# Interleaving the two experts of a pair, chunk by chunk, in a mixture-of-experts stage

## The chip, the cores and the metric

The kernel runs as one launch on one core of a Trainium2 chip. The metric is the device time in microseconds: 1492.72 us, the median of three runs (1490.94, 1492.72 and 1494.07).

## The reference, and what is computed

Two layers of a decoder for 256 tokens of width 1024, in float32. Layer 0 is a mixer of RWKV-7 and forgetting attention with a dense SwiGLU behind it; layer 1 is a causal convolution module with a mixture of experts behind it. Only the last part matters here:

```python
logits = xt @ w_router                       # 256 tokens, 8 experts
top_v, top_i = lax.top_k(logits, 2)          # two experts for each token
for e in range(8):                           # hidden width 3584
    y = y + gates[:, e:e+1] * (silu(xt @ w_gate[e]) * (xt @ w_up[e])) @ w_down[e]
```

Each expert has three matrices of 1024 x 3584 float32, so all eight have 352 MB of weights, which are read once. A token goes to two experts of eight, so an expert sees 64 tokens on average; how many each sees is known only when the router has run.

## The kernel before, in words

**Stages.** Layer 0 and the convolution take the first 575 us of the profiled execution. The expert stage (method `moe`, from L1357 on) takes the rest.

**Loads.** A weight matrix is cut into 7 chunks of 512 hidden columns; a chunk of one matrix is two loads of 1 MiB (L1221 to L1230). All loads are issued by SyncE in the program's order into a ring of 12 buffers (`wx`, `wt`, `wr`), so a load waits until what lay in its buffer has been read.

**Experts by size.** Expert 0 goes first, alone. The other seven are sorted by their number of tokens. The largest, `big`, is computed with split float32r operands: each 1 MiB load is cut into two parts, and `parts` (L1264) makes a high half `bh` on ScalarE (L197) and from it a low half `bl` on VectorE (L198). Its work is 21 *phases*, 7 chunks times gate, up and down, with two loads each; on TensorE a phase is 96 matmuls of L1279 or 48 of L1298 to L1300. The other six form three pairs of a heavier and a lighter expert: (1, 2), (3, 4) and (5, 6) in the kernel's numbering `n`. For each pair a branch picks an *arm* by the counts. In the profiled execution the arms are: expert 0 with up to 64 rows (`HALF`); the first and the last pair with up to 96 rows and up to 32 rows (`MOST` and `FEW`); the middle pair with up to 64 rows each (`HALF`, `HALF`).

**A chunk of an expert.** `project` for gate and for up (L1233; 64-row matmuls on L1243, 32-row ones on L1250), `silu` on ScalarE (L1310), then `down` of the chunk *before* it (L1325; 64-row sums on L1336, 32-row sums on L1342), then `hidden` (L1314): the product on VectorE (L1316), a transpose on TensorE (L1319), and a copy of the transposed rows from PSUM to SBUF on ScalarE (L1321). That copy's target, `ht`, is taken from two rotating buffers (L1320, `self.tmp(self.mo, [P, 512], "ht", 2)`); `down` of the next chunk reads it. So each call of `hidden` takes the buffer that the call before the last one had.

**Sums.** The 64-row sums of an expert are in the PSUM bank `yp[0]`, its 32-row sums in `yp[1]` (MOST) or `yp[0]` (FEW). At an expert's end `evac` (L1204) copies them to `yh` and `yl`, one piece after the other: ScalarE writes a piece of `yh` (L197), VectorE the same piece of `yl` (L198). `scatter` (L1189) multiplies `yh` and `yl` with a one-hot matrix and adds the result to the output rows on VectorE (L1197). `gather` (L1157) makes an expert's rows from the tokens with another one-hot matrix.

**Order.** The order of the work on every engine is the program's, with small moves that the framework's scheduler makes when the kernel is built. Expert after expert is done; the phases of `big` stand at chunks named by a table `extra`: of the first pair one phase at the heavier expert and six at the lighter one, of the middle pair four and three, of the last pair one and six. The scatter of an expert stands in the first chunks of the next one, its gather in a middle chunk of the one before.

Of the kernel before, what the change touches and what calls it, by code (L numbers as in the profile page):

```python
# [11 lines left out]
F32R = mybir.dt.float32r  # L12
# [6 lines left out]
P = 128  # L19
T = 256  # L20
# [3 lines left out]
NE = 8  # L24
# [3 lines left out]
FULL, MOST, HALF, FEW = "full", "most", "half", "few"  # L28
# [84 lines left out]
class Trunk:  # L113
# [242 lines left out]
    def pair(self, tag, bufs=1):  # L356
        return self.tmp(self.l0, [P, 2, T], tag, bufs)
# [987 lines left out]
    def moe(self):  # L1345
        nc, tc, a = self.nc, self.tc, self.a
        nch = NCH
# [34 lines left out]
        xe = [self.xx[0][:, :, P * i : P * i + P].bitcast(F32) for i in range(2)]  # L1382
        xb = [self.xx[1], mo.tile([P, NK, T], F32R, name="xbl", bufs=1)]
        sb = [one(f"sb{b}", [P, 512]) for b in range(2)]
        self.bh = [mo.tile([P, 1024], F32R, name="bh" + q, bufs=1) for q in "hl"]
        oht = [mo.tile([P, T], F32R, name=f"oht{i}", bufs=1) for i in range(5)]


        turn = [None, 1, 6, 3, 4, 2, 5]
        exs = []  # L1390
        for n, r in enumerate(turn):
            gate, pos = self.first if r is None else (self.sgate[:, :, r : r + 1], self.spos[:, :, :, r : r + 1])
            exs.append(dict(n=n, e=0, gate=gate, pos=pos, x=[xe[n % 2], xe[(n + 1) % 2]], o=[oht[n % 3], oht[(n + 2) % 3]]))
        blk = lambda b: tuple(t[:, :, P * b : P * b + P] for t in xb)
        big = dict(n=NE, xs=xb, gate=self.sgate[:, :, 0:1], pos=self.spos[:, :, :, 0:1], x=[blk(0), blk(1)], o=oht[3:])
        self.gather(exs[0], 0)
        cols = lambda t: [t[:, 512 * hf : 512 * hf + 512] for hf in range(2)]


        def arm(n, mode, hooks, b=0, first=True, phases=True):  # L1400
            me = exs[n]
            if b:
                me = dict(me, x=me["x"][1:])
            if not first:
                me = dict(me, n=NE)
            for c in range(nch + 1):
                if c < nch:
                    s = self.silu(mode, self.project(me, "g", c, mode, load))
                    up = self.project(me, "u", c, mode, load)
                elif phases:  # L1410
                    phase(n, nch - 1)
                if c > 0:
                    ws = [load(me, "d", c - 1, i) for i in range(2)]
                    self.down(mode, h, ws, yp, c == 1, c == nch)
                if c < nch:
                    h = self.hidden(mode, s, up)
                if c in hooks:
                    hooks[c]()
                if c < nch - 1 and phases:
                    phase(n, c)  # L1420
            self.evac(mode, yp)

        def phase(n, c):
            if c not in extra.get(n, ()):
                return
            k = sum(len(v) for j, v in extra.items() if j < n) + extra[n].index(c)
# [30 lines left out]

        yp = [self.mpsum("yp", "y") for _ in range(2)]
        form = value(self.cnt0[0:1, 0:1], 2)
        extra = {1: (6,), 2: (0, 1, 2, 3, 4, 6), 3: (0, 2, 4, 6), 4: (1, 3, 5), 5: (6,), 6: (0, 1, 2, 3, 4, 5)}  # L1460

        def hooks(n, first, last, prev):
            h = {}
            ph = extra.get(n, ()) if last else ()
            if prev is not None:
                h[next((c for c in ph if c < nch - 1), 0)] = prev
            if n == 0 and first:
                h[1] = ranks
                h[2] = lambda: self.gather(big, 0)
                h[3] = lambda: self.gather(big, 1)  # L1470
            if last and n < len(exs) - 1:
                at = [c for c in ph if 3 <= c < nch - 1 and c not in h]
                h[at[0] if at else 4] = lambda: self.gather(exs[n + 1], 0)
            elif last:
                h[2] = last_rows
            return h


        TWO = (FULL, FULL)
        sets = [((0,), [((HALF,),), ((FULL,),), (TWO,)])]  # L1480
        sets += [((i, i + 1), arms) for i, arms in (
            (1, [((MOST,), (FEW,)), ((FULL,), (HALF,)), (TWO, (FULL,))]),
            (3, [((HALF,), (HALF,)), ((FULL,), (FULL,))]),
            (5, [((MOST,), (FEW,)), ((FULL,), (HALF,)), (TWO, (FULL,))]))]
        NS = NE - 1
        for s, (members, arms) in enumerate(sets):
            w0 = wi[0]

            def go(j):
                wi[0] = w0  # L1490
                for n, modes in zip(members, arms[j]):
                    prev = (lambda n=n: self.scatter(exs[n - 1], 0)) if n > 0 else None
                    if len(modes) == 2:
                        if prev is not None:
                            prev()
                        self.gather(exs[n], 1)
                        arm(n, modes[1], hooks(n, True, False, None), 1, True, False)
                        prev = lambda n=n: self.scatter(exs[n], 1)
                    first = len(modes) == 1
                    arm(n, modes[0], hooks(n, first, True, prev), 0, first)  # L1500
# [133 lines left out]
```

## Time and profile before

| | |
|---|---|
| median of three runs | 1492.72 us |
| the profiled execution, its own time | 1493.51 us |
| its span, first to last instruction | 1491.7 us |
| mean granted TensorE clock | 0.976 of full speed |
| TensorE busy | 1399.1 us (94%) |
| VectorE / ScalarE busy | 575.2 us (39%) / 450.8 us (30%) |
| read from memory | 422.81 MB |

The span is what lies between the first and the last instruction on the engines; the time of the run has 1.8 us around it. Shares of busy time are averages over stages with different limits, so the expert stage is read by itself. TensorE is the engine whose work is longest there, and the loads are near the rate that they reach anywhere (about 420 GB/s) in most of it. Two kinds of idle time tell them apart: if TensorE waits for a load, the row of that wait names a DMA; if the loads wait for buffers, their rate falls.

### The profile page before, as it was taken

What the parts mean: (1) busy time and instruction counts of PE and PEld (TensorE: products, weight loads), DVE (VectorE), ACT (ScalarE), POOL (GpSimd) and SP (SyncE); (2) the same over time, 40 slices, a digit from 0 to 9 for tenths busy, and PEclk for the clock granted to TensorE, in tenths of its full rate; (3) what the DMA queues carried; (4) which work ended last, traced back from release to release, by engine and by line L of the source; (5) the groups of instructions that cost most, each with busy time, mean ns of one, the idle gap of its engine ahead of it and who ended that gap; (6) DMA issues with size and microseconds to landing.
All of it is one profiled execution on the core that took longest, in us unless ns stands there. A gap on an engine that the chain in (4) does not pass through costs nothing. (4 is left out here: it accounts for less than half of the span.)

```text
span 1491.7 us, 32344 instructions
## 1 busy us (share of the span) xinstructions
PE 1399.1 (94%) x14162; PEld 1050.8 (70%) x14162; DVE 575.2 (39%) x980; ACT 450.8 (30%) x747; POOL 37.8 (3%) x63
## 2 busy tenths in 40 slices
PE   6999998999979998998999999899999989999995
PEld 5877777999966775655667787766656656668882
DVE  2865437655587664201002423321231210024435
ACT  5443435444447662110002222211212100013231
POOL 1100010000001100000000000000000000000000
PEclk7999999999989998999999999999999999999997
DMA  6331144555634236999998999899999999999992
GB/s 232 118 111 61 55 141 150 190 189 180 195 87 135 69 112 256 420 399 411 418 388 321 405 417 391 342 419 420 419 420 419 409 359 372 351 348 356 419 417 110
DMA packets 107208, 426.23 MB, mean 286 GB/s; under 512 B 6842, under 2 KB 55994, under 8 KB 64032
## 3 DMA queue, kind: packets, MB, share of 16 engines
q1 hardware_dynamic: 105968, 420.15, 73.0%
q0 software_dynamic: 1072, 3.74, 0.7%
q8 instruction: 118, 1.93, 0.5%
q14 instruction: 50, 0.41, 0.1%
HBM read 422.81 MB, written 1.05 MB: 284 GB/s over the span
## 5 line engine op out<-in xcount | busy, mean ns | idle before, releaser
L172 DVE TENSOR_TENSOR wl<-w,wh 128x1024 fp32r<-128x1024 f32 x122 | 150.3, 1235 | 126.1 <-ACT wh L170 125.5
L170 ACT ACTIVATE wh<-w 128x1024 fp32r<-128x1024 f32 x122 | 128.8, 1059 | 156.1 <-PE gu L209 55.3
L1316 DVE TENSOR_TENSOR sl<-sl,gu 128x256 f32<-128x256 f32 (+2 forms) x49 | 20.7, 421 | 391.0 <-PE gu L1243 347.2
L1279 PE MATMUL gu<-xl,bl 128*128 128x256 f32 x448 | 126.5, 287 | 6.2 <-DVE bl L198 6.0
L1279 PE MATMUL gu<-xl,bh 128*128 128x256 f32 x448 | 126.2, 283 | 1.4 <-ACT bh L197 1.4
L1279 PE MATMUL gu<-xbl,bh 128*128 128x256 f32 x448 | 126.2, 283 | 0.0
L1243 PE MATMUL gu<-wr,xh 128*64 128x256 f32 x1024 | 116.9, 381 | 6.2 <-issue 3.2
L1243 PEld LDWEIGHTS gu<-wr,xh 128*64 128x64 f32 x1024 | 72.9, 137 | 45.0 <-issue 8.3
L1321 ACT ACTIVATE ht<-ht 128x256 f32<-128x256 f32 (+2 forms) x49 | 18.8, 384 | 282.4 <-PE ht L1319 282.4
L208 PE MATMUL gu<-xh,wh 128*128 128x256 f32 x352 | 99.5, 284 | 1.6 <-DVE nt L825 1.6
L210 PE MATMUL gu<-xh,wl 128*128 128x256 f32 x352 | 99.3, 283 | 0.4 <-DVE wl L172 0.4
L209 PE MATMUL gu<-xl,wh 128*128 128x256 f32 x352 | 99.3, 283 | 0.0
L1243 PE MATMUL gu<-wt,xh 128*64 128x256 f32 x768 | 90.3, 382 | 0.4 <-issue 0.4
L1279 PEld LDWEIGHTS gu<-xl,bl 128*128 128x128 f32 x448 | 84.0, 190 | 8.7 <-DVE bl L198 8.7
L1279 PEld LDWEIGHTS gu<-xl,bh 128*128 128x128 f32 x448 | 85.3, 190 | 5.5 <-issue 3.7
L1279 PEld LDWEIGHTS gu<-xbl,bh 128*128 128x128 f32 x448 | 85.1, 190 | 0.2
L1243 PEld LDWEIGHTS gu<-wt,xh 128*64 128x64 f32 x768 | 53.9, 137 | 30.9 <-issue 6.4
L1310 ACT ACTIVATE sl<-gu 128x256 f32<-128x256 f32 (+2 forms) x49 | 18.8, 385 | 185.9 <-PE gu L1250 110.5
L1336 PE MATMUL yp<-wr,ht 128*64 128x512 f32 x304 | 69.8, 595 | 0.5 <-ACT ht L1321 0.5
L208 PEld LDWEIGHTS gu<-xh,wh 128*128 128x128 f32 x352 | 67.0, 191 | 2.7 <-DVE nt L825 1.7
L198 DVE TENSOR_TENSOR bl<-wr,bh 128x1024 fp32r<-128x1024 f32 x40 | 48.2, 1223 | 51.3 <-ACT bh L197 51.3
L210 PEld LDWEIGHTS gu<-xh,wl 128*128 128x128 f32 x352 | 67.0, 190 | 0.6 <-DVE wl L172 0.6
(438 smaller groups left out, 2677.6 us busy)
## 6 DMA issues: line engine op xcount, KB each, us to landing
wr<-in_wd_dram SPq DMA_DIRECT2D x58, 1024.0 KB, 13.2
wr<-in_wg_dram SPq DMA_DIRECT2D x56, 1024.0 KB, 13.7
wr<-in_wu_dram SPq DMA_DIRECT2D x52, 1024.0 KB, 13.6
wt<-in_wg_dram SPq DMA_DIRECT2D x44, 1024.0 KB, 11.4
wt<-in_wd_dram SPq DMA_DIRECT2D x40, 1024.0 KB, 15.0
wx<-in_wu_dram SPq DMA_DIRECT2D x32, 1024.0 KB, 12.6
wt<-in_wu_dram SPq DMA_DIRECT2D x28, 1024.0 KB, 10.5
wx<-in_wd_dram SPq DMA_DIRECT2D x14, 1024.0 KB, 9.1
```

The source lines that it names most:

```text
L170: self.split_act = nc.scalar.activation(wh, w[:, k : k + g], AF.Copy)
L172: self.split_ins = nc.vector.tensor_tensor(wl, w[:, k : k + g], wh.bitcast(F32), op=ALU.subtract)
L198: nc.vector.tensor_tensor(lo, src, hi.bitcast(F32), op=ALU.subtract)
L208: nc.tensor.matmul(ps, wh[:, cols], xh[:, k], start=first and k == 0, stop=False, skip_group_check=True)
L209: nc.tensor.matmul(ps, wh[:, cols], xl[:, k], start=False, stop=False, skip_group_check=True)
L210: nc.tensor.matmul(ps, wl[:, cols], xh[:, k], start=False, stop=k == NK - 1, skip_group_check=True)
L1243: nc.tensor.matmul(p[64 * h : 64 * h + 64, :T], x[:, kk, 0:64], w[:, T * h : T * h + T], start=st and not up, stop=sp, tile_position=(0, 6 ...
L1279: mm = lambda l, r, st, sp: nc.tensor.matmul(o, l[:, k, cols], r[:, kk], start=st, stop=sp, skip_group_check=True)
L1310: self.nc.scalar.activation(s[:, :w], gate[:, :w], AF.Silu)
L1316: self.last_mul = nc.vector.tensor_tensor(s[:, :w], s[:, :w], up[:, :w], op=ALU.mult)
L1321: nc.scalar.activation(h[:, :w], ps[:, :w], AF.Copy)
L1336: nc.tensor.matmul(y[0][64 * d : 64 * d + 64], h[:, o : o + 64], w[:, 512 * d : 512 * d + 512], start=st, stop=sp, tile_position=(0, 64 * ...
```

## The change

The lighter expert of a pair is no longer done after the heavier one. A new function `joint` does chunk c of the heavier expert, then chunk c of the lighter one, then one phase of `big`, and so on through the chunks (a *double chunk*). It is used by the arms that these inputs take (MOST with FEW, HALF with HALF); the other arms keep the old sequence with other places for phases and gathers. Each pair now has 7 phases spread over its chunks: in the first two pairs one at each of chunks 0 to 5 and one ahead of the last `down`; in the last pair two at chunk 0 and one at each of chunks 1 to 5. The FEW expert's sums go to the upper half of the columns of `yp[1]`, whose lower half holds the MOST expert's last 32 rows; in the middle pair they go to `yp[1]`. The two experts' rows must both be there when a pair begins, so the gathers stand one pair earlier, and the scatter of the heavier expert stands at the end of its own pair. The one-hot matrices get a sixth buffer.

The diff, cut to its core:

```diff
-        oht = [mo.tile([P, T], F32R, name=f"oht{i}", bufs=1) for i in range(5)]
+        oht = [mo.tile([P, T], F32R, name=f"oht{i}", bufs=1) for i in range(6)]
...
+        def step(me, mode, c, h, y, opens=True):
+            if c < nch:
+                s = self.silu(mode, self.project(me, "g", c, mode, load))
+                up = self.project(me, "u", c, mode, load)
+            if c > 0:
+                ws = [load(me, "d", c - 1, i) for i in range(2)]
+                self.down(mode, h, ws, y, c == 1 and opens, c == nch)
+            return self.hidden(mode, s, up) if c < nch else None
...
+        def joint(members, modes, hooks, phases):
+            n, m = members
+            yb = [yp[1][:, T:]] if modes[1] == FEW else [yp[1]]
+            ha = hb = None
+            for c in range(nch + 1):
+                if c == nch:
+                    for k in phases[c]:
+                        phase(k)
+                ha = step(exs[n], modes[0], c, ha, yp)
+                if c == nch:
+                    self.evac(modes[0], yp)
+                hb = step(exs[m], modes[1], c, hb, yb, modes[1] != FEW)
+                if c in hooks:
+                    hooks[c]()
+                if c < nch:
+                    for k in phases[c]:
+                        phase(k)
+            self.scatter(exs[n], 0)
+            self.evac(modes[1], yb)
...
-        extra = {1: (6,), 2: (0, 1, 2, 3, 4, 6), 3: (0, 2, 4, 6), 4: (1, 3, 5), 5: (6,), 6: (0, 1, 2, 3, 4, 5)}
...
+        def pair(s, members, modes):
+            n, m = members
+            k = 7 * (s - 1)
+            h = {0: lambda: self.scatter(exs[n - 1], 0)}
+            if m < len(exs) - 1:
+                h[nch - 1] = lambda: self.gather(exs[m + 1], 0)
+                h[nch] = lambda: self.gather(exs[m + 2], 0)
+                ph = [(k + c,) for c in range(6)] + [(), (k + 6,)]
+            else:
+                h[2] = last_rows
+                ph = [(k, k + 1)] + [(k + c + 1,) for c in range(1, 6)] + [(), ()]
+            joint(members, modes, h, ph)
...
+                if isinstance(arms[j][0], str):
+                    pair(s, members, arms[j])
+                else:
+                    sequence(s, members, arms[j])
```

Three places show what this does to the order of instructions. The first is TensorE in the first pair, at a chunk of the FEW expert that a phase follows. Before, chunk 2 of that expert (`gu` are its projections, `ht` the transposes and, as an input, the SBUF copy; `yp` the sums):

```order
L1250 MATMUL gu_8951<-wr_5531,xh_5551 32x128 x16
L1250 MATMUL gu_8988<-wx_5515,xh_5551 32x128 x16
L1250 MATMUL gu_8988<-wx_5516,xh_5551 32x128 x16
L1319 MATMUL ht_9042<-cstT,sl_8986 128x128
L1342 MATMUL yp_5673<-wt_5517,ht_8875 32x256 x8
L1342 MATMUL yp_5673<-wt_5518,ht_8875 32x256 x8
L1279 MATMUL gu_9046<-xl_5552,bh_9050 128x256
```

Now, chunk 1 of that expert, with a chunk of the MOST expert ahead of it:

```order
L1319 MATMUL ht_7970<-cstT,sl_7890 128x128 x3
L1250 MATMUL gu_7976<-wt_5519,xh_5551 32x128 x16
L1250 MATMUL gu_7976<-wt_5520,xh_5551 32x128 x16
L1250 MATMUL gu_8013<-wr_5526,xh_5551 32x128 x16
L1250 MATMUL gu_8013<-wr_5527,xh_5551 32x128 x16
L1319 MATMUL ht_8067<-cstT,sl_8011 128x128
L1342 MATMUL yp_5675<-wr_5528,ht_7703 32x256 x8
L1342 MATMUL yp_5675<-wr_5529,ht_7703 32x256 x8
L1279 MATMUL gu_8071<-xl_5552,bh_8075 128x256
```

The FEW expert's own rows stand in the same order in both: projections, transpose, the sums of the chunk before, then the phase, whose first matmul reads `bh`. What stands ahead of them has changed.

The second place is ScalarE at the same chunks (L1310 silu, L1321 the copy to `ht`, L197 the high halves for the phase). Before, two chunks of the FEW expert that follow each other:

```order
L1310 ACTIVATE sl_8986<-gu_8951 128x128
L1321 ACTIVATE ht_9044<-ht_9042 128x128
L197 ACTIVATE bh_9050<-wt_5519 128x1024
L197 ACTIVATE bh_9078<-wt_5519 128x1024
L197 ACTIVATE bh_9106<-wt_5520 128x1024
L197 ACTIVATE bh_9134<-wt_5520 128x1024
L1439 ACTIVATE sb_5637<-gu_9046 128x512
L1439 ACTIVATE sb_5638<-gu_9047 128x512
L1310 ACTIVATE sl_9199<-gu_9164 128x128
L1321 ACTIVATE ht_9257<-ht_9255 128x128
```

Now, from the FEW expert's copy of chunk 0 to its copy of chunk 1:

```order
L1321 ACTIVATE ht_7703<-ht_7701 128x128
L197 ACTIVATE bh_7725<-wr_5528 128x1024
L197 ACTIVATE bh_7753<-wr_5528 128x1024
L197 ACTIVATE bh_7781<-wr_5529 128x1024
L197 ACTIVATE bh_7809<-wr_5529 128x1024
L1459 ACTIVATE sb_5637<-gu_7721 128x512
L1459 ACTIVATE sb_5638<-gu_7722 128x512
L1310 ACTIVATE sl_7890<-gu_7839 128x384
L1321 ACTIVATE ht_7974<-ht_7970 128x384
L1310 ACTIVATE sl_8011<-gu_7976 128x128
L1321 ACTIVATE ht_8069<-ht_8067 128x128
L197 ACTIVATE bh_8075<-wr_5530 128x1024
```

Between two copies of one expert (7703 and 8069) there is now one of the other expert (7974); before there was none (9044, then 9257). In both, the high halves of a phase stand behind the expert's copy.

The third place is TensorE at the end of the last pair (`sca` are the scatters). Before, the FEW expert's last sums and, behind the branch, its scatter:

```order
L1342 MATMUL yp_5673<-wr_5528,ht_18547 32x256 x8
L1342 MATMUL yp_5673<-wr_5529,ht_18547 32x256 x8
L1319 MATMUL ht_18754<-cstT,sl_18698 128x128
L1342 MATMUL yp_5673<-wr_5530,ht_18756 32x256 x8
L1342 MATMUL yp_5673<-wr_5531,ht_18756 32x256 x8
```

Now, from the MOST expert's last sums on:

```order
L1336 MATMUL yp_5674<-wr_5529,ht_18689 64x512 x4
L1342 MATMUL yp_5675<-wr_5529,ht_18689 32x256 x8
L1196 MATMUL sca_18842<-yh,oht_5642 128x512
L1196 MATMUL sca_18842<-yl,oht_5642 128x512
L1196 MATMUL sca_18846<-yh,oht_5642 128x512
L1196 MATMUL sca_18850<-yh,oht_5642 128x512
L1196 MATMUL sca_18850<-yl,oht_5642 128x512
L1342 MATMUL yp_5675<-wr_5530,ht_18784 32x256 x8
L1342 MATMUL yp_5675<-wr_5531,ht_18784 32x256 x8
L1196 MATMUL sca_18846<-yl,oht_5642 128x512
```

The scatter of the MOST expert stands directly behind that expert's last sums, ahead of the last sums of the FEW expert.

## Rows read from the trace of the kernel before

**Rows 1.** Engines by stretch: length, PE, PEld, DVE, ACT, POOL, clock, DMA, GB/s.
```profile
678.40:813.00 134.60, 133.59 (x1807) 87.66 (x1807) 13.22 (x21) 13.07 (x22) 0.00 (x0) 1.00 0.97 393
...
944.80:1207.60 262.80, 248.79 (x1808) 167.15 (x1808) 64.08 (x82) 49.68 (x75) 0.00 (x0) 1.00 1.01 416
1207.60:1342.70 135.10, 133.61 (x1759) 85.65 (x1759) 15.40 (x22) 11.87 (x20) 0.00 (x0) 1.00 0.92 352
...
sum 889.50, PE 851.32 PEld 598.26 DVE 213.66 ACT 166.95 POOL 0.00; mean PE 141.89 PEld 99.71 DVE 35.61 ACT 27.82 POOL 0.00
```

**Rows 2.** Waits of TensorE, 583 to 1492 us: total us, times, longest.
```profile
PE ht L1319 <- DVE sl L1316: 12.0, 21, 0.8
PE gu L1243 <- issue: 6.9, 4, 3.2
PE gu L1279 <- DVE bl L198: 6.0, 6, 1.2
...
PE y L1299 <- DVE bl L198: 2.4, 3, 1.5
...
PE gu L1279 <- ACT bh L197: 1.4, 1, 1.4
```

**Rows 3.** As rows 1: a MOST chunk, then a FEW chunk with its phase.
```profile
1240.50:1257.10 16.60, 16.60 (x247) 10.24 (x243) 0.56 (x1) 0.98 (x2) 0.00 (x0) 1.00 0.97 372
1404.77:1422.96 18.19, 17.64 (x257) 15.98 (x257) 5.10 (x5) 5.76 (x8) 0.00 (x0) 1.00 1.01 418
```

**Rows 4.** In order of time, a FEW chunk into its phase: start, us, engine, line.
```profile
1404.77 0.33 PE L1319 MATMUL ht<-cstT,sl 128*128 128x128 f32 x1 [0.48 <-DVE sl L1316]
...
1405.03 1.93 PE L1342 MATMUL yp<-wr,ht 128*32 128x256 f32 x32
1405.13 0.28 ACT L1321 ACTIVATE ht<-ht 128x128 f32<-128x128 f32 x1 [2.25 <-PE ht L1319]
1405.31 1.99 ACT L197 ACTIVATE bh<-wr 128x1024 fp32r<-128x1024 f32 x2
...
1406.89 0.38 PE L1279 MATMUL gu<-xl,bh 128*128 128x256 f32 x1
...
1407.67 0.39 PE L1279 MATMUL gu<-xl,bl 128*128 128x256 f32 x1
```

**Rows 5.** The same for a HALF chunk into a phase.
```profile
987.21 3.65 PE L1336 MATMUL yp<-wx,ht 128*64 128x512 f32 x16
...
987.32 0.38 ACT L1321 ACTIVATE ht<-ht 128x256 f32<-128x256 f32 x1 [4.09 <-PE ht L1319]
...
990.79 0.73 PE L1298 MATMUL y<-bh,bhh 128*128 128x512 f32 x2
...
991.36 0.40 PE L1299 MATMUL y<-bl,bhh 128*128 128x512 f32 x1
```

**Rows 6.** TensorE, two phases that begin right behind a scatter.
```profile
823.73 0.39 PE L1279 MATMUL gu<-xl,bl 128*128 128x256 f32 x1 [1.03 <-DVE bl L198]
...
1104.58 0.51 PE L1299 MATMUL y<-bl,bhh 128*128 128x512 f32 x1 [1.52 <-DVE bl L198]
```

**Rows 7.** TensorE, a phase that begins right behind a gather.
```profile
883.49 0.38 PE L1279 MATMUL gu<-xl,bh 128*128 128x256 f32 x1 [1.42 <-ACT bh L197]
...
884.75 0.38 PE L1279 MATMUL gu<-xl,bl 128*128 128x256 f32 x1 [0.53 <-DVE bl L198]
```

**Rows 8.** As rows 1, the 3.4 us behind rows 7.
```profile
885.40:888.80 3.40, 3.40 (x18) 3.40 (x17) 0.42 (x1) 0.09 (x1) 0.00 (x0) 0.50 1.02 422
```

**Rows 9.** In order of time, the evacuation of a MOST expert, first and last pieces.
```profile
1342.84 0.59 ACT L197 ACTIVATE yh<-yp 64x512 fp32r<-64x512 f32 x1 [8.13 <-PE yp L1336]
...
1344.48 3.68 PE L1250 MATMUL gu<-wr,xh 128*32 128x128 f32 x128
...
1348.12 0.43 DVE L198 TENSOR_TENSOR yl<-yp,yh 32x256 fp32r<-32x256 f32 x1 [0.44 <-ACT yh L197]
```

More of the change, by code (lines that the diff above doesn't have):

```diff
@@ L1392, in moe, with arm @@
             gate, pos = self.first if r is None else (self.sgate[:, :, r : r + 1], self.spos[:, :, :, r : r + 1])
-            exs.append(dict(n=n, e=0, gate=gate, pos=pos, x=[xe[n % 2], xe[(n + 1) % 2]], o=[oht[n % 3], oht[(n + 2) % 3]]))
+            exs.append(dict(n=n, e=0, gate=gate, pos=pos, x=[xe[n % 2], xe[(n + 1) % 2]], o=[oht[n % 4], oht[(n + 2) % 4]]))
         blk = lambda b: tuple(t[:, :, P * b : P * b + P] for t in xb)
-        big = dict(n=NE, xs=xb, gate=self.sgate[:, :, 0:1], pos=self.spos[:, :, :, 0:1], x=[blk(0), blk(1)], o=oht[3:])
+        big = dict(n=NE, xs=xb, gate=self.sgate[:, :, 0:1], pos=self.spos[:, :, :, 0:1], x=[blk(0), blk(1)], o=oht[4:])
         self.gather(exs[0], 0)
         cols = lambda t: [t[:, 512 * hf : 512 * hf + 512] for hf in range(2)]
-        def arm(n, mode, hooks, b=0, first=True, phases=True):
+        def step(me, mode, c, h, y, opens=True):
[6 more added lines that the diff above has]
+            return self.hidden(mode, s, up) if c < nch else None
+        def arm(n, mode, hooks, b=0, first=True, phases=()):
             me = exs[n]
@@ L1405, in arm, with phase @@
                 me = dict(me, n=NE)
+            h = None
             for c in range(nch + 1):
[L1407 to L1416, printed above, removed]
+                h = step(me, mode, c, h, yp)
                 if c in hooks:
                     hooks[c]()
-                if c < nch - 1 and phases:
-                    phase(n, c)
+                for k in phases[c] if c < len(phases) else ():
+                    phase(k)
             self.evac(mode, yp)
[L1423 to L1426, printed above, removed]
+        def joint(members, modes, hooks, phases):
[14 more added lines that the diff above has]
+                    for k in phases[c]:
+                        phase(k)
+            self.scatter(exs[n], 0)
+            self.evac(modes[1], yb)
+        def phase(k):
             cc, kind = k // 3, "gud"[k % 3]
@@ L1459, in moe @@
         form = value(self.cnt0[0:1, 0:1], 2)
-        extra = {1: (6,), 2: (0, 1, 2, 3, 4, 6), 3: (0, 2, 4, 6), 4: (1, 3, 5), 5: (6,), 6: (0, 1, 2, 3, 4, 5)}
[L1462 to L1476, printed above, removed]
         TWO = (FULL, FULL)
@@ L1481, in moe, with sequence @@
         sets += [((i, i + 1), arms) for i, arms in (
-            (1, [((MOST,), (FEW,)), ((FULL,), (HALF,)), (TWO, (FULL,))]),
-            (3, [((HALF,), (HALF,)), ((FULL,), (FULL,))]),
-            (5, [((MOST,), (FEW,)), ((FULL,), (HALF,)), (TWO, (FULL,))]))]
+            (1, [(MOST, FEW), ((FULL,), (HALF,)), (TWO, (FULL,))]),
+            (3, [(HALF, HALF), ((FULL,), (FULL,))]),
+            (5, [(MOST, FEW), ((FULL,), (HALF,)), (TWO, (FULL,))]))]
+        def sequence(s, members, arms):
+            last = members[-1]
+            k = 7 * (s - 1)
+            for j, (n, modes) in enumerate(zip(members, arms)):
+                prev = (lambda n=n: self.scatter(exs[n - 1], 0)) if n > 0 else None
+                if len(modes) == 2:
+                    if prev is not None:
+                        prev()
+                    self.gather(exs[n], 1)
+                    h = {1: ranks, 2: lambda: self.gather(big, 0), 3: lambda: self.gather(big, 1)} if n == 0 else {}
+                    arm(n, modes[1], h, 1)
+                    prev = lambda n=n: self.scatter(exs[n], 1)
+                first = len(modes) == 1
+                h = {} if prev is None else {0: prev}
+                if n == 0 and first:
+                    h.update({1: ranks, 2: lambda: self.gather(big, 0), 3: lambda: self.gather(big, 1)})
+                if n == 0:
+                    h.update({4: lambda: self.gather(exs[1], 0), nch - 1: lambda: self.gather(exs[2], 0)})
+                ph = [(), (), (), ()] + [()] * 4 if n == 0 else [(k,), (), (k + 1,), (), (k + 2,)] if j == 0 else \
+                    [(k,), (k + 1,), (k + 2,), (), (k + 3,)]
+                arm(n, modes[0], h, 0, first, ph)
+                k += 3
+                if len(modes) == 2 and n != last:
+                    self.gather(exs[n + 1], 0)
+            if 0 < last < len(exs) - 1:
+                for i in (1, 2):
+                    self.gather(exs[last + i], 0)
+            elif last > 0:
+                last_rows()
@@ new lines, in pair @@
+        def pair(s, members, modes):
+            n, m = members
+            k = 7 * (s - 1)
+            h = {0: lambda: self.scatter(exs[n - 1], 0)}
[7 more added lines that the diff above has]
+            joint(members, modes, h, ph)
@@ L1490, in go @@
                 wi[0] = w0
[L1491 to L1500, printed above, removed]
+                if isinstance(arms[j][0], str):
+                    pair(s, members, arms[j])
+                else:
+                    sequence(s, members, arms[j])
             def choose(j):
```

## The prediction, made before the changed kernel was run

> **What bounds the kernel now.** I read the engines by stretch first. The expert stage lasts 889.5 us and TensorE is busy for 851.3 of them, so 38.2 us are idle [rows 1]. The loads run at 352 to 416 GB/s in the pairs [rows 1], below the 418 of a FEW chunk with its phase [rows 3], so they have something in reserve but not much. Which of the two ends last is told by the waits of TensorE, read next: the large ones name VectorE's `sl`, the branches between sets, and the splits `bh` and `bl`; none of those in the expert stage names a DMA [rows 2]. So TensorE bounds the stage, and the loads wait for buffers.
>
> Then I read one chunk of each kind. A MOST chunk without a phase takes 16.60 us and TensorE is busy in all of it; a FEW chunk with a phase takes 18.19 us [rows 3]. A double chunk is therefore 34.8 us of TensorE and 14 loads of 1 MiB (six for each expert, two for the phase). At the 418 GB/s of the FEW chunk these take 14 x 1.049 MB / 0.418 = 35.1 us. That is about equal, so both limits have to be looked at.
>
> Last I read the start of a phase in order of time. In a FEW chunk the transpose starts at 1404.77, ScalarE's copy to `ht` follows at 1405.13, and the phase's `bh` splits follow the copy at 1405.31, all while TensorE does the 16 sums `yp` from 1405.03 to 1406.96 [rows 4]. The phase starts at 1406.89 and its first `bl` matmul at 1407.67: the sums cover the copy and the first splits, almost to the nanosecond.
>
> **The change, part by part.** The matmuls are the same in number and shape, so what changes is waits. The sum is made against the profiled execution's 1493.5 us, 0.8 above the median.
>
> *The copy to `ht`.* `ht` has two buffers, and each call of `hidden` takes the one of the call before the last. Before, that one belonged to the same expert two chunks earlier, long read. Now calls of the two experts alternate, so the lighter expert's copy takes the buffer of its own chunk before, and the sums that read this one stand behind the transposes on TensorE: in the order shown for TensorE, `ht_8067` is made, then `yp` reads `ht_7703`, then the phase begins. The copy `ht_8069` must wait until those sums end. ScalarE works in order, and `bh_8075` stands right behind the copy; VectorE's `bl` needs `bh`; and the phase needs both. So the cover of the 16 sums is gone.
>
> For FEW the copy moves from 1405.13 to the end of the sums at 1406.96, plus 0.03 for the handover (an estimate): 1406.99, or 1.86 later. The first `bl` matmul stood 2.54 us behind the copy (1407.67 - 1405.13) and is the last to be late, so the phase loses 1.86, about 1.3 in front of the first `bh` matmul and the rest in front of the first `bl` [rows 4]. It happens at chunks 1 to 5 of the first pair and 2 to 5 of the last: 9 x 1.86 = 16.7. At chunk 1 of the last pair I take 1.4. For HALF the sums run from 987.21 to 990.86; the copy was at 987.32 and the first `bl` matmul behind it could have been 2.64 us later, but stood at 991.36 because the sums were in front [rows 5]. Now it is 990.89 + 2.64 = 993.53, 2.17 late; five chunks give 10.9. Together 29.0 us. The heavier expert's copy is held back in the same way, but a whole projection stands between it and the next need: nothing.
>
> From below the cost is zero, if the copy doesn't have to wait. From above each place loses the whole cover, 1.93 or 3.65 us [rows 4, 5]: 10 x 1.93 + 5 x 3.65 = 37.6. I take 29.0, since the chain of durations is in the rows.
>
> *Waits that go.* The nine waits for `bl` and the one for `bh` are 9.8 us in the named rows [rows 2], and about 10.1 with a small one beside them. They are where a scatter or a gather puts work of ScalarE and VectorE ahead of a split, as 1.03 and 1.52 behind scatters and 1.42 + 0.53 behind a gather [rows 6, 7]. There are fewer of these places, because the phases now stand elsewhere: three behind scatters (1.0 to 1.5) and two behind gathers (1.1 and 1.3) remain by the order, 6.4. That is -3.7. Single `ht` waits in the FEW chunks give -0.9. The 12.0 us for `sl` [rows 2] recur once per chunk in either order: 0 (their end would be 0 to -12, if the other expert's work came between product and transpose; in the order it does not).
>
> *Ends of the pairs.* The MOST expert's evacuation is a chain of ScalarE and VectorE from 1342.84 to 1348.55, 5.7 us, and before it lay beside the next projections, which begin at 1344.48 [rows 9]. Now the scatter that reads it stands right behind the expert's last sums. Beside the chain lie the 32-row sums, 1.9, and what the scatter can do on the first half of the columns, about 1.2; that leaves 2.6 of wait. Behind the FEW expert's last sums three more scatter matmuls stand, some 0.4 each, and the FEW evacuation must wait for them because it writes the same `yh` and `yl`: 1.3. So 3.9 in the last pair; in the first, matmuls of a gather stand ahead of the scatter, some 0.8, so 3.1. In the middle pair the evacuation has two pieces, less than half the chain, beside the other expert's 3.65 us of sums [rows 5]: 0. Together +7.0, between 0 and 11 (both chains bare).
>
> *The rest.* The four branch waits (6.9) [rows 2] stay. One gather more stands in expert 0 and one less behind; their matmuls are moved, at 0. The loads are issued in a new order, with MOST and FEW loads alternating. Each double chunk takes 34.8 + 1.9 = 36.7 us of TensorE against 35.1 of loads, so the ring of 12 fills and no DMA ends a wait: 0. If TensorE were not held back, 0.3 x 13 = 4 us would appear here. The sixth one-hot buffer adds no instruction: 0.
>
> Sum: 29.0 - 3.7 - 0.9 + 7.0 = +31.4, less some 0.3 for chunk 0 of FEW. 1493.5 + 31.1 = 1524.6, and by the median 1523.8. I say 1524.
>
> **A rule against the trace.** After one wait of 1.42 us and another of 0.53 [rows 7] the trace has 3.4 us with the granted clock at 0.50, that is 1.2 instead of 2.4 GHz [rows 8]; other waits as long, the 1.52 at 1104.58 among them [rows 6], have no such stretch behind them. The Trainium skill, page "TensorE: Matmul & The Clock Gate", section "A second HAM failure mode: psum-queue depth-cycling", tells of a kernel whose short pauses between groups of matmuls, coming again and again, let the clock fall and recover, at the cost of throughput. Rows 7 and 8 agree with it once; the 1.52 us wait and the branch waits disagree. By the rule each of the 15 new waits would carry such a stretch, which is the third rival below; by the trace they carry one in ten, 1.7 us or so, which is the forecast.
>
> **Rivals.**
>
> *Faster: the loads are what the kernel waits for.* The rate in the MOST stretch is 352 to 393 and in the FEW stretch 418 [rows 1, 3], and the change levels it. If MOST chunks were stretched by something of the loads that no wait names, each of 14 would go from 16.60 to about 15.0, the time of its 6 loads at 418: -22, and 1471. Against it: TensorE is busy in 16.60 of 16.60 us [rows 3].
>
> *No difference: the copy isn't held.* If the buffer is free early after all, only the other terms stay: 1493.5 + 7.0 - 4.9 = 1495.6, or 1495. For it: nothing in the trace shows such a wait now. Against it: the order of the rows on TensorE and the count of two buffers.
>
> *Much slower: the clock.* Each of 15 waits is followed by 3.4 us at half the clock, which loses 1.7: +25, and 1550. For it rows 7 and 8; against it rows 6. It decides from about five such stretches on.
>
> **How the numbers follow.** The forecast has 0.76, the clock rival 0.10, the faster one 0.09, no difference 0.05. A measurement of this kernel can tell 0.2%, some 3 us, from no change. The forecast's own range is 1507 to 1537: below, half of the copies' waits are covered by something and the ends cost 4; above, each place loses its whole cover and the ends 11. With the clock taken in partly, 1506 to 1546. Slower is 0.76 + 0.10 = 0.86; faster 0.09; within 0.2% 0.05.
>
> **What will show it.** ScalarE's copy at L1321 should wait for `yp` at L1342 and L1336 of TensorE, not for `ht`. TensorE's waits for `bh` should grow from 1.4 to about 20 us, in some 15 places of 1.3 to 1.5, and those for `bl` by some 12 there. A double chunk should take about 36.7 us, and the rate in the pairs should be level at 380 to 400 GB/s with no DMA among the waits of TensorE. At the ends of the first and the last pair the scatter should wait for `yh` by two to three us. The forecast is wrong if copies start within 0.4 us behind their transposes, if a DMA ends waits of TensorE, or if the clock in the pairs is under 0.97.

## The result, and the profile of the changed kernel

The changed kernel takes 1546.78 us (median of four runs, 1543.12 to 1548.52), the kernel before 1491.83: a ratio of 1.0367, 95% interval 1.0348 to 1.0385. It is slower, as forecast, but by 55 us where 31 were forecast. That is 9.8 us above the forecast's own range (1507 to 1537), and 0.8 above the wider one with the clock taken in partly.

The expert stage by sets, in the columns of [rows 1], from the first projection to TensorE's last matmul:

```profile
585.40:680.67 95.27, 92.55 (x710) 57.24 (x711) 14.84 (x58) 14.89 (x31) 0.00 (x0) 1.00 0.96 383
680.67:963.10 282.43, 263.31 (x3488) 195.06 (x3488) 61.88 (x80) 50.00 (x78) 0.00 (x0) 0.96 0.92 366
963.10:1242.80 279.70, 254.44 (x1810) 171.58 (x1810) 64.97 (x84) 50.49 (x77) 0.00 (x0) 0.97 0.95 386
1242.80:1528.90 286.10, 265.92 (x3396) 188.69 (x3396) 71.16 (x92) 51.88 (x79) 0.00 (x0) 0.96 0.83 331
sum 943.50, PE 876.23 PEld 612.57 DVE 212.85 ACT 167.27 POOL 0.00; mean PE 219.06 PEld 153.14 DVE 53.21 ACT 41.82 POOL 0.00
```

Before, the sum was 889.50 with 851.32 busy [rows 1]. Of the 54.0 us more, 29.1 are idle time of TensorE (67.3 against 38.2) and 24.9 are busy time of the same matmuls. The third number from the end of a row says why: the granted clock is 0.96 to 0.97 in the pairs, where it was 0.99 to 1.00. In time, 58.0 us of the stage run at half the clock, where it was 6.8; with TensorE busy in most of them that loses 25.6 us against 3.3, which is 22.3 of the 24.9. So there are two costs of about one size, and the forecast's sum had only the first.

The waits of TensorE, which answer to [rows 2]:

```profile
PE gu L1279 <- ACT bh L197: 12.4, 9, 1.4
PE ht L1319 <- DVE sl L1316: 12.2, 21, 1.5
PE gu L1279 <- DVE bl L198: 8.5, 12, 1.5
PE y L1298 <- ACT bh L197: 8.2, 6, 1.4
PE sca L1196 <- ACT yh L197: 7.6, 4, 2.7
PE gu L1243 <- DMA wr<-in_wd_dram: 6.0, 1, 6.0
PE y L1299 <- DVE bl L198: 4.7, 7, 1.5
```

`bh` has 20.6 us in 15 places, where it had 1.4 in one and 0.3 in another. Fourteen of the 15 follow the lighter expert's held-back copy; the fifteenth, at chunk 1 of the last pair, has another reason: there the sums stand ahead of the transposes, so that nothing covers copy and splits. One of the fourteen in order of time, the FEW expert's chunk 1 in the first pair; its rows answer to [rows 4]:

```profile
735.34 1.93 PE L1342 MATMUL yp<-wr,ht 128*32 128x256 f32 x32
...
737.34 0.28 ACT L1321 ACTIVATE ht<-ht 128x128 f32<-128x128 f32 x1 [4.14 <-PE yp L1342]
737.52 1.99 ACT L197 ACTIVATE bh<-wr 128x1024 fp32r<-128x1024 f32 x2
...
738.62 0.38 PE L1279 MATMUL gu<-xl,bh 128*128 128x256 f32 x1 [1.34 <-ACT bh L197]
...
739.88 0.45 PE L1279 MATMUL gu<-xl,bl 128*128 128x256 f32 x1 [0.52 <-DVE bl L198]
740.13 0.42 PE L1279 MATMUL gu<-xl,bh 128*128 128x256 f32 x1
```

The copy to `ht` now waits for the sums `yp` (in brackets), ends up 2.0 us behind their start where it was 0.1, and the splits and the phase follow it: 1.34 + 0.52 = 1.86 us. Then look at the length of the last two matmuls: 0.45 and 0.42 us, where the ones ahead of the wait took 0.28. The clock has fallen. In a HALF chunk [rows 5] the same waits are 1.43 and 0.53:

```profile
1015.31 3.65 PE L1336 MATMUL yp<-wt,ht 128*64 128x512 f32 x16
...
1019.01 0.39 ACT L1321 ACTIVATE ht<-ht 128x256 f32<-128x256 f32 x1 [7.68 <-PE yp L1336]
...
1020.39 0.73 PE L1298 MATMUL y<-bh,bhh 128*128 128x512 f32 x2 [1.43 <-ACT bh L197]
1021.65 0.50 PE L1299 MATMUL y<-bl,bhh 128*128 128x512 f32 x1 [0.53 <-DVE bl L198]
```

The 3.4 us behind four such places, to be read against [rows 8]:

```profile
740.00:743.40 3.40, 3.40 (x17) 3.40 (x18) 0.96 (x1) 0.00 (x0) 0.00 (x0) 0.51 1.01 419
778.20:781.60 3.40, 3.40 (x15) 2.76 (x16) 0.96 (x1) 0.89 (x1) 0.00 (x0) 1.00 1.01 419
815.40:818.80 3.40, 3.40 (x19) 3.40 (x18) 0.54 (x1) 0.00 (x0) 0.00 (x0) 0.54 1.01 424
853.60:857.00 3.40, 3.40 (x31) 3.40 (x30) 0.84 (x2) 1.06 (x1) 0.00 (x0) 1.00 1.00 417
```

TensorE is busy in all of each, but in the first and third at about half the clock. Of the 15 places 8 have such a stretch behind them, 1.7 us each: 13.6 us. The other stretches stand at two branches (4.6 us lost) and at the ends of the first and the last pair (7.4).

### The profile page after: what moved, and what is told of

Its sections match the earlier page's. It is cut to its first block, busy times and chain, and to the rows that moved or that the text cites. A ratio compares the mean times of both kernels' runs of the same rounds, so it can differ in the third digit from the quotient of the medians.

```text
span 1544.3 us, 32341 instructions
## 1 busy us (share of the span) xinstructions
PE 1423.5 (92%) x14162; PEld 1067.0 (69%) x14162; DVE 574.1 (37%) x980; ACT 450.4 (29%) x747; POOL 37.7 (2%) x63
## 5 line engine op out<-in xcount | busy, mean ns | idle before, releaser
L1316 DVE TENSOR_TENSOR sl<-sl,gu 128x256 f32<-128x256 f32 (+2 forms) x49 | 20.6, 421 | 435.7 <-PE gu L1243 320.9
L1279 PE MATMUL gu<-xl,bl 128*128 128x256 f32 x448 | 130.4, 296 | 8.5 <-DVE bl L198 8.5
L1243 PE MATMUL gu<-wr,xh 128*64 128x256 f32 x1056 | 126.5, 388 | 7.4 <-DMA wr<-in_wd_dram 6.0
L1243 PEld LDWEIGHTS gu<-wr,xh 128*64 128x64 f32 x1056 | 76.3, 139 | 50.6 <-issue 10.8
L1321 ACT ACTIVATE ht<-ht 128x256 f32<-128x256 f32 (+2 forms) x49 | 18.8, 385 | 316.3 <-PE ht L1319 231.8
L1279 PEld LDWEIGHTS gu<-xl,bh 128*128 128x128 f32 x448 | 88.7, 198 | 17.8 <-ACT bh L197 17.6
L1279 PEld LDWEIGHTS gu<-xl,bl 128*128 128x128 f32 x448 | 88.1, 199 | 11.0 <-DVE bl L198 11.0
L1279 PEld LDWEIGHTS gu<-xbl,bh 128*128 128x128 f32 x448 | 88.6, 198 | 0.2
L198 DVE TENSOR_TENSOR bl<-wr,bh 128x1024 fp32r<-128x1024 f32 x44 | 53.0, 1223 | 79.6 <-ACT bh L197 79.6
L1243 PE MATMUL gu<-wt,xh 128*64 128x256 f32 x704 | 80.6, 381 | 0.0
L1310 ACT ACTIVATE sl<-gu 128x256 f32<-128x256 f32 (+2 forms) x49 | 18.8, 385 | 190.3 <-PE gu L1250 113.7
L209 PEld LDWEIGHTS gu<-xl,wh 128*128 128x128 f32 x352 | 67.6, 192 | 0.7 <-DVE xl L826 0.3
L1243 PEld LDWEIGHTS gu<-wt,xh 128*64 128x64 f32 x704 | 49.9, 137 | 26.0 <-issue 2.6
```

What stands on the lines that cost most here:

```text
L198: nc.vector.tensor_tensor(lo, src, hi.bitcast(F32), op=ALU.subtract)
L209: nc.tensor.matmul(ps, wh[:, cols], xl[:, k], start=False, stop=False, skip_group_check=True)
L1243: nc.tensor.matmul(p[64 * h : 64 * h + 64, :T], x[:, kk, 0:64], w[:, T * h : T * h + T], start=st and not up, stop=sp, tile_position=(0, 6 ...
L1279: mm = lambda l, r, st, sp: nc.tensor.matmul(o, l[:, k, cols], r[:, kk], start=st, stop=sp, skip_group_check=True)
L1310: self.nc.scalar.activation(s[:, :w], gate[:, :w], AF.Silu)
L1316: self.last_mul = nc.vector.tensor_tensor(s[:, :w], s[:, :w], up[:, :w], op=ALU.mult)
```

## The experiments

Theory A, formed on these rows: the copies held back by the sums make TensorE wait at 15 phase starts, 28 us; about half of the waits pull the clock down, 13.6 us; the rest stands at the ends of the pairs. Rival B: the clock falls for a reason of its own. Rival C: the interleaving itself costs the time, by its loads or its order.

**Own `ht` columns.** One tile for a double chunk, its columns shared out between the two experts, so that a copy's target was last read two sums earlier:

```diff
-                ha = step(exs[n], modes[0], c, ha, yp)
+                ht, w = self.tmp(self.mo, [P, 512], "ht", 2) if c < nch else None, WIDE[modes[0]]
+                ha = step(exs[n], modes[0], c, ha, yp, True, ht[:, :w] if c < nch else None)
...
-                hb = step(exs[m], modes[1], c, hb, yb, modes[1] != FEW)
+                hb = step(exs[m], modes[1], c, hb, yb, modes[1] != FEW, ht[:, w:] if c < nch else None)
```

> The changed kernel, with one `ht` tile for a double chunk: the heavier expert's transposed rows lie in its first columns, the lighter one's behind them, so no copy waits for the sums of the chunk before. Theory A (the held-back copies make TensorE wait at 15 phase starts, 28 us, and 8 of these waits are followed by 1.7 us lost at half the clock, 13.6): 1546.8 - 28 - 13.6 = about 1505. Rival B (the clock falls for reasons of its own, not because of these waits): 1546.8 - 28 = about 1519. Rival C (the time is lost by the interleaving itself, by loads or by the ends of the pairs): about 1545.

Measured: 1504.15 us, 1.0077 of before (1.0049 to 1.0106). The waits for `bh` are down to one:

```profile
PE ht L1319 <- DVE sl L1316: 11.8, 21, 1.1
PE sca L1196 <- ACT yh L197: 8.6, 5, 2.6
PE gu L1243 <- DMA wr<-in_wd_dram: 6.0, 1, 6.0
PE gu L1279 <- DVE bl L198: 4.3, 4, 1.5
...
PE gu L1279 <- ACT bh L197: 1.3, 1, 1.3
```

That one is the place at chunk 1 of the last pair, where no buffer is waited for. Between the half-clock stretches at the two ends of the first pair the clock holds 1.00 (first row), where the changed kernel had 0.98 (second row):

```profile
684.60:940.60 256.00, 247.40 (x3430) 185.21 (x3426) 58.23 (x72) 49.38 (x76) 0.00 (x0) 1.00 0.95 388
685.40:951.00 265.60, 249.52 (x3411) 187.40 (x3408) 54.84 (x67) 47.86 (x72) 0.00 (x0) 0.98 0.92 371
```

Over whole pairs it is 0.99, 0.99 and 0.97: the stretches at branches and ends remain, and one behind the `bh` wait that is left. The time is theory A's number; B's (1519) and C's (1545) are out. One edit to a buffer takes back 43 of the 55 us.

**The copy behind the splits.** The two alternating buffers stay; on ScalarE the lighter expert's copy goes behind the phase's first two splits:

```diff
             wh, wl = self.parts(ws[n // 2][:, 2 * (n % 2) : 2 * (n % 2) + 2])
+            if n == 1 and late:
+                with self.tc.issue_after(self.last_hi.ins):
+                    late.pop()()
```

> The changed kernel with its two alternating `ht` buffers, but on ScalarE the lighter expert's copy is issued behind the first two `bh` splits of the phase. The copy still waits for the sums. Theory A (it is ScalarE's order that hands the wait on to the phase): the waits for `bh` go as in the version with own buffers, about 1505 to 1510. Rival (TensorE needs the copy itself early, or the buffer holds something else): 1540 or more.

Measured: 1499.24, 1.0044 (1.0022 to 1.0067); no wait for `bh` is left in the trace. That is 6 us below the expected 1505, and far from the rival's 1540. So the wait for the buffer does no harm by itself. It is ScalarE's order that hands it on to the splits, as the prediction had it.

**TensorE kept busy in the wait.**

```diff
+                if 0 < c < nch - 1 and phases[c]:
+                    fill = self.mpsum("fill", "t")
+                    with tc.issue_after(self.last_sum.ins):
+                        for _ in range(10):
+                            nc.tensor.matmul(fill[:, :T], xb[0][:, 0, :P], xb[0][:, 1], start=True, stop=True, skip_group_check=True)
                 if c < nch:
                     for k in phases[c]:
                         phase(k)
```

> The changed kernel with ten matmuls more, of 128 columns by 256, ahead of each phase that follows the lighter expert's sums; their result is not read. They fill most of the 1.34 or 1.43 us in which TensorE waits for `bh`, so the wait itself stays and only TensorE's idleness goes; the 0.5 us wait for `bl` behind it stays. Theory A (the clock falls because TensorE idles): the half-clock stretches behind these waits go, 8 x 1.7 = 13.6, so about 1533. Rival B (the clock falls for another reason): about 1547. If the added matmuls stand in the way: over 1550.

Measured: 1541.57, 1.0326 (1.0290 to 1.0362): 5 us less than the changed kernel, not 14. The clock did what A expected. Two stretches of 10 us around phase starts of the changed kernel, and the same of this one:

```profile
735.00:745.00 10.00, 8.05 (x67) 6.73 (x68) 2.39 (x3) 3.21 (x4) 0.00 (x0) 0.83 1.01 415
811.00:821.00 10.00, 8.11 (x67) 7.16 (x60) 3.33 (x3) 3.23 (x4) 0.00 (x0) 0.83 1.01 419
```

```profile
735.00:745.00 10.00, 8.99 (x96) 7.31 (x88) 3.44 (x4) 3.23 (x4) 0.00 (x0) 1.00 1.01 415
811.00:821.00 10.00, 9.48 (x78) 8.97 (x75) 4.28 (x4) 4.29 (x5) 0.00 (x0) 1.00 1.02 423
```

None of the 15 phase starts has a half-clock stretch any more, although each still waits 0.52 us for `bl`. Most of what took the rest back is at the first branch behind a pair:

```profile
PE gu L1243 <- issue: 8.6, 1, 8.6
```

Where the changed kernel waited 0.9 us there, this one waited 8.6, with the code around that branch the same; why is not known. At the phase starts, idleness is what pulls the clock down (B is out). The waits at branches differ by several us from kernel to kernel.

**The wait without the interleaving.** In the kernel before, one buffer for `ht` (`"hs", 1` in place of `"ht", 2` at L1320).

> The kernel before, not interleaved, with one `ht` buffer for the experts in place of two (its tile is named `hs`): each copy waits for the sums of its expert's chunk before. Theory A: at 9 FEW and 5 HALF chunks a phase follows, 9 x 1.87 + 5 x 1.96 = 26.6, and about half of the waits bring 1.7 us of half clock, 12: 1491.8 + 39 = about 1531. Without the clock 1518. Rival C (the interleaving is what costs): about 1492.

Measured: 1521.75, 1.0203 (1.0172 to 1.0235). The same rows as in the changed kernel appear, in experts that are not interleaved:

```profile
857.37 0.28 ACT L1321 ACTIVATE hs<-ht 128x128 f32<-128x128 f32 x1 [4.11 <-PE yp L1342]
857.55 1.99 ACT L197 ACTIVATE bh<-wt 128x1024 fp32r<-128x1024 f32 x2
...
858.65 0.39 PE L1279 MATMUL gu<-xl,bh 128*128 128x256 f32 x1 [1.34 <-ACT bh L197]
...
859.90 0.45 PE L1279 MATMUL gu<-xl,bl 128*128 128x256 f32 x1 [0.52 <-DVE bl L198]
```

The wait was there at 12 places, not 14 (at two of the five HALF chunks a scatter or a gather stands between), and 3 of the 12 brought half clock, not half of them. So it is 28 us where A said 39 and C said none. The wait alone does it; how often the clock follows is not the same in each kernel.

**Splits and loads issued early.** On top of the own columns, a phase's loads and first two splits go ahead of the lighter expert's chunk:

```diff
+                if c < nch - 1 and phases[c]:
+                    ahead(phases[c][0])
                 hb = step(exs[m], modes[1], c, hb, yb, modes[1] != FEW, ht[:, w:] if c < nch else None)
```

> As the version with one `ht` tile for a double chunk, and the loads and the first two splits of a phase are issued ahead of the lighter expert's chunk (or of the gather), not behind its scatter, copy or gather. Theory A (what is left between 1504 and 1493 are waits for splits, 7.1 us by its trace, and the ends of the pairs): the 7.1 go, about 1497, or 1495 with some clock. Rival (loads bound it: two ring buffers are held a chunk longer, and DMA waits appear on TensorE): 1505 or more.

Measured: 1504.37, 1.0088 (1.0071 to 1.0105). The time is the rival's, not A's 1497, and loads now end waits:

```profile
PE sca L1196 <- ACT yh L197: 8.8, 5, 2.7
PE gu L1243 <- DMA wr<-in_wu_dram: 8.5, 3, 6.0
PE ht L1326 <- DVE sl L1323: 4.2, 7, 0.7
...
PE gu L1243 <- DMA wr<-in_wg_dram: 1.4, 3, 0.6
PE gu L1250 <- DMA wt<-in_wu_dram: 1.4, 1, 1.4
PE gu L1286 <- DVE bl L198: 1.2, 1, 1.2
```

The waits for splits go, from 7.1 to 1.2 us, and those for `sl` fall from 11.8 to 4.2; in their place loads end waits of 6.3 us inside the pairs and one of 6.0 at a branch. A double chunk without waits is 34.8 us of TensorE against 35.1 of loads, so there is little left for TensorE to save here. Yet the loads are not shown to be the whole reason: TensorE's idle time in the stage fell from 41.7 to 34.3 us, and its busy time rose from 860.6 to 868.2 with the same matmuls and about the same loss at half clock (11.1 and 11.7 us). What made them longer is open.

**Ends inside the lighter expert's last chunk.** On top of that, the heavier expert's last sums and its evacuation go between the two projections of the lighter one's last chunk, its scatter ahead of the lighter one's last sums:

```diff
+                    s = self.silu(modes[1], self.project(exs[m], "g", c, modes[1], load))
+                    step(exs[n], modes[0], nch, ha, yp)
+                    self.evac(modes[0], yp)
+                    up = self.project(exs[m], "u", c, modes[1], load)
```

> As the version with early splits, and the heavier expert's last sums and evacuation stand between the two projections of the lighter one's last chunk, its scatter ahead of the lighter expert's last sums. Theory A (the uncovered evacuations at the ends cost some 6 us of waits and some 3 to 5 us of half clock): 1495 - 10 = about 1486, below the kernel before. Rival C (the interleaving costs time by itself): no better than 1493.

Measured: 1503.40, 1.0076 (1.0055 to 1.0097): not A's 1486. The scatters' waits for `yh` fell from 8.8 to 2.2 us as expected, but at the ends of the first and the last pair the transposes now wait 2.6 and 2.5 us for `sl`, which gives most of it back; two branches cost 10.7 us, and loads still end waits. What comes ahead of the stage, which is the same code, took some 5 us longer in the profiled execution; the stage itself is 898.9 us against 902.5 in the experiment before it.

**Early splits without the interleaving.** The same in the kernel before, its splits and loads ahead of the expert's sums.

> The kernel before, not interleaved, with the loads and first two splits of a phase issued ahead of the expert's sums, scatter or gather. Theory A (a phase start waits wherever ScalarE has other work ahead of its splits): the waits for `bl` and `bh`, 9.8 us, go, but for those at places where the phase stands ahead of the last sums (2.3), and the one half-clock stretch, 1.7: about 1483. Rival (the splits then stand in the way of something else on ScalarE or VectorE): 1492.

Measured: 1515.95, 1.0173 (1.0141 to 1.0206): a miss. The scheduler put the sums ahead of the transposes, so the transposes stand right before the phase and the splits behind the copy:

```profile
857.98 0.33 PE L1326 MATMUL ht<-cstT,sl 128*128 128x128 f32 x1 [0.48 <-DVE sl L1323]
858.35 0.28 ACT L1328 ACTIVATE ht<-ht 128x128 f32<-128x128 f32 x1 [2.22 <-PE ht L1326]
858.52 1.99 ACT L197 ACTIVATE bh<-wt 128x1024 fp32r<-128x1024 f32 x2
...
859.62 0.38 PE L1286 MATMUL gu<-xl,bh 128*128 128x256 f32 x1 [1.31 <-ACT bh L197]
```

So it doesn't tell what early splits are worth. It shows the mechanism from the other side: no copy is held back, but the sums no longer cover copy and splits, and the wait is 1.31 us, as with a held copy (1.34).

**Splits first and ends.** The edits of the second and the sixth experiment together.

> As the version with the copy behind the first two splits (1499), and the heavier expert's last sums and evacuation between the two projections of the lighter one's last chunk, its scatter ahead of the lighter expert's last sums. Theory A (the uncovered evacuations of the interleaving are what is left): the scatters' waits for `yh` fall from 7.6 to about 2.3 us, and about 3 us of half clock behind them go: 1499 - 8 = about 1491, no worse than the kernel before. Rival C (the interleaving costs time by itself): about 1499.

Measured: 1495.38, 1.0017 (0.9998 to 1.0036), between A's 1491 and C's 1499, so it does not decide between them. The scatters' waits fell to 2.6 us, but a transpose at the end of the first pair waits 2.5 for `sl`, and the three branches wait 4.6, 5.6 and 5.8 us, against 2.9 to 3.2 before.

**Not-taken arms made longer.** In the changed kernel SyncE issues the last load of the middle set by 1193.5 and the first one of the last set at 1216.88 (view of the DMA issues in order of time, SyncE's queue):

```profile
1187.96 5.49 SPq L1230 DMA_DIRECT2D wr<-in_wd_dram  x4
1216.88 1.88 SPq L1230 DMA_DIRECT2D wr<-in_wg_dram  x2
1219.08 1.35 SPq L1230 DMA_DIRECT2D wx<-in_wu_dram  x2
```

Its buffer had been read by 1197. The edit adds matmuls to code that does not run:

```diff
+                pad = self.mpsum("pad", "t")
+                for _ in range({1: 200, 2: 120}[s]):
+                    nc.tensor.matmul(pad[:, :P], xb[0][:, 0, :P], xb[0][:, 1, :P], start=True, stop=True, skip_group_check=True)
```

> The changed kernel, with 200 and 120 matmuls more at the ends of arms that are not taken here, in the first and middle sets; nothing that runs is changed. Theory D: SyncE issues the last set's first load 24 us after its last one (1193.1, then 1216.9), because a load behind a branch waits for a count of TensorE's instructions that must hold whichever arm was taken, and in the other arm of the middle pair the buffer is read later, counted from the end; with matmuls added behind that read the count falls by 102. Then the load goes out about 19 us earlier, the burst of loads at the branch goes, TensorE's wait of 6.0 us at 1242.8 falls to about 3, and some 2 us of half clock with it: about 1541 to 1542. Rival: the loads were held by something else: 1547.

Measured: 1549.89, 1.0382 (1.0353 to 1.0412), with runs from 1540.24 to 1554.30. The load goes out as expected:

```profile
1185.64 5.49 SPq L1230 DMA_DIRECT2D wr<-in_wd_dram  x4
1196.75 1.00 SPq L1230 DMA_DIRECT2D wr<-in_wg_dram  x2
1198.08 0.99 SPq L1230 DMA_DIRECT2D wx<-in_wu_dram  x2
```

TensorE's wait at that branch fell from 6.0 to 3.5 us (in the profiled run, the shortest of the six), but the time of the kernel does not show it and is nearer to the rival's 1547 than to 1542: its runs spread over 14 us, the shortest at a mean clock of 0.966 and the longest at 0.958, which is 13 us at this length. That code which is not run holds this load back is shown; what it is worth in this kernel is not.

**Both.** Splits first, ends, and the longer arms.

> Both of the other two edits together: copy behind the first splits, ends inside the lighter expert's last chunk, and the matmuls at the ends of the arms that are not taken. Theory A with D: 1491 - 5 = about 1486, faster than the kernel before (about 1491). Rival: the waits at the branches only move: 1491.

Measured: 1490.09 against 1492.59, 0.9996 (0.9975 to 1.0017): no difference from the kernel before, in 12 runs. Theory A with D had said 1486 and was wrong; the rival, with waits at the branches that only move, had said 1491. The last set's first load left 20 us earlier than in the eighth experiment, but TensorE still waits 4.4, 5.5 and 5.4 us at the three branches. The stage is 890.5 us long with TensorE busy for 853.6, against 889.5 and 851.3 [rows 1]. So with the waits that it brought taken out, the interleaving costs nothing and brings nothing; rival C is out, and no version here is faster than the kernel before.

## Where the prediction was right, and where it failed

*What bounds the kernel* held. TensorE waits for no load inside the pairs of the changed kernel; the one wait that names a DMA is at a branch. But the prediction had called itself wrong if a DMA ended a wait of TensorE or if the clock in the pairs was under 0.97, and both came: the 6.0 us at the branch, and 0.96. The rate of the loads was to be level at 380 to 400 GB/s and is 366, 386 and 331 in the three pairs.

*The copy to `ht`* held in mechanism and size. It was put at 29.0 us; the 15 places show 20.6 for `bh` and about 0.53 each for `bl` behind it, 28.5. (The waits for `bl` there were to grow by some 12 and are 8.) A FEW place was put at 1.86 and has 1.86 of idle time. A HALF place was put at 2.17 and has 1.96 of idle time; from the start of the sums to the first `bl` matmul it takes 6.34 us where it took 4.15 [rows 5], 2.19 more. A double chunk was put at 36.7 us, and in the first pair the phases follow each other after 36.7 and 36.8 where the clock held. The second experiment shows the queue on ScalarE to be the link.

*The waits that go* were put at 9.8 less 6.4 left. Behind scatters and a gather 5.3 us of `bl` are left. The place at chunk 1 of the last pair, taken at 1.4, is among the 15 above with 1.83.

*The ends* were put at +7.0. The waits of the scatters for `yh` are 7.6 us, of which 2.5 at the very end of the last pair were there before, so it is about +5; the waits for `oht`, `oh` and `xh` of the gathers there add some 2.

*The rest* at nothing held in its sum, though not branch by branch. The row read as "four branch waits (6.9)" [rows 2] has two of them, 2.9 and 3.2, and two waits of 0.4 inside a set; the third branch wait, 3.0, stands in another row. The three are 9.0 us before and 2.1, 0.9 and 6.0, again 9.0, in the changed kernel. The 6.0 stands where the last set's loads left late. That a load behind a branch is tied to arms that are not taken was not in the reading at all, but how much of the 6.0 it makes is open: with the loads 20 us earlier this wait fell to 3.5 in the ninth experiment, and in the tenth it was 5.4 against 5.8 in the eighth.

*The clock* is the step that failed. The idle time was forecast at 31.1 us more and came out at 29.1. For the clock the text allowed "one in ten" waits, 1.7 us in all, and the sum has no term for it at all. It is most of the 24.9 us of busy time: 13.6 behind 8 of the 15 new waits, and 12.0 at branches and at the ends of the pairs, in stretches of 3.4 to 10.2 us, less the 3.3 of before. Some 2.6 us of the 24.9 lie outside the half-clock stretches. The rival that had each of 15 waits followed by 1.7 us gave 1550, nearest to the measured 1547, and it was given a chance of 0.10. Its number is luck in part: 8 of the 15 waits had a stretch, and the rest of its 25 us came from branches and ends, which it did not name.

The rows held more than the working took from them. Of the waits for splits before, six were single ones of 0.96 to 1.52 us, for `bl` alone (two of them in [rows 6]), and none of them had a half-clock stretch behind it. One was a pair, 1.42 for `bh` and 0.53 for `bl` 1.3 us later [rows 7], and it did [rows 8]. (A small pair, 0.31 and 0.53, did not.) The 15 new waits were forecast as pairs of the form of [rows 7], so the row to go by was the one like them, not the average over all. The changed kernel says the same: its single waits of 1.04 to 1.51 us behind scatters and a gather have no such stretch, the pairs have one in 8 of 15. Over all twelve traces, 27 of 53 such pairs have one, and none of 39 single waits for `bl` of 0.96 to 1.52 us. That both waits of a pair are needed is not shown: in the seventh experiment the clock is at 0.50 from 1179.1, behind a wait of 1.42, and the second wait of that pair begins at 1179.36. With half of 15 at 1.7 us the forecast would have been 1524 + 13 = 1537; the stretches at ends and branches make most of the rest. What picks the 8 from the 15 is open. In the first pair it is every second one.

A second half-clock stretch of before was not weighed. It stands at the scatter that waits 2.47 us for `yh` at the end of the last pair:

```profile
1472.50:1475.90 3.40, 3.28 (x8) 2.44 (x8) 0.70 (x2) 0.64 (x2) 0.00 (x0) 0.50 0.04 10
```

The change adds waits of this form at the ends of the first and the last pair, and the 7.4 us of half clock there go with them.

The rule of the Trainium skill, "TensorE: Matmul & The Clock Gate", section "A second HAM failure mode: psum-queue depth-cycling", that short pauses between groups of matmuls, coming again and again, cost throughput through the clock, agrees with these runs in part: with the pauses filled, the clock stays at 1.00 in the two stretches shown, but the single pauses of 0.96 to 1.52 us have no half clock behind them.

## What to carry to other kernels

When two streams of work share a rotating buffer, count the ring again: an alternation halves its depth for each stream, and a copy that waits for it holds up whatever stands behind it on its engine. A new wait on an engine that was always busy is charged twice, once for the wait and once for the clock that may fall behind it; to price the second, look for a wait of the same form in the trace, even if there is only one. And where TensorE bounds the stage and no wait names a load, a new order that spreads the loads better had nothing to win here: the best interleaved version ended level with the old one.

## What the runs showed of the hardware

- The same matmuls of one phase take 0.28 us each at full clock and 0.41 to 0.42 at half clock behind a pair of waits; the stretch is 3.4 us long at a phase start, and costs 1.7 us.
- Filling 1.3 us of waiting with ten matmuls whose result is not used keeps the clock up and costs nothing where TensorE would have waited anyway: in the first pair the phases then follow each other after 36.6 to 36.7 us, as they do unfilled where the clock held (36.7 and 36.8), against 38.2 where it fell.
- TensorE's wait at a branch between two sets was anything from 0.6 to 8.6 us over these kernels; at one branch, with the code around it the same, 0.9 and 8.6. What sets it wasn't found.
- Code in an arm that isn't taken moved the issue of a load that does run by 20 us.
